# Single block pairs in the triangular inverse, a halved last doubling, opening loads in fewer pieces and moved activations

## The chip, the cores and the metric

One core of a Trainium2 chip runs the whole program once; the metric is the device time of that run in microseconds. The matrix work is done by TensorE (PE in the profile; PEld is its weight load), element work by VectorE (DVE), ScalarE (ACT) and a little by GpSimd (POOL). Transfers from device memory are issued by SyncE (SP) and by ScalarE.

## The reference

A sequence of 256 tokens of width 1024 goes through two layers of one kind and one layer of another, all in float32:

```python
for l in range(2):
    h = rms_norm(x, norm_mix[l]); proj = h @ w_in[l]          # 12 dilated heads, 4 stick-breaking heads, gates
    y_a = dilated_attention(dq, dk, dv) @ w_proj_a[l]
    y_b = stick_breaking_attention(sq, sk, sv) @ w_proj_b[l]
    x = x + (gates_a * y_a + gates_b * y_b) @ w_out[l]
    x = x + conv_ffn(rms_norm(x, norm_ffn[l]), ...)           # 1024 -> 2*2816 -> 1024
x = rms_norm(x, norm_final)
proj = rmsnorm(x) @ w_in_2
...
i_plus_a = a_low + eye(64)                                    # gated delta rule, chunks of 64 tokens, 4 heads
sol = triangular_solve(i_plus_a, rhs, lower=True)
...
mix = concat([rmsnorm(o, gdn_norm_w) * silu(z), lru_out])     # delta rule and RG-LRU
x = x + mix @ w_out_2
x = x + relu(rmsnorm(x) @ w_ff1) ** 2 @ w_ff2
return rmsnorm(x, final_norm_w)
```

## The kernel before

Every large product is made of three matmuls in a reduced float format: the weights and the streamed activations are each split into a rounded part and the rest, `wh` and `wl` for weights, `xh` and `xl` for activations. A weight block of 1 MB comes by one transfer into `raw` (L135); ScalarE writes `wh` as the rounded copy (L148, 128x1024), VectorE writes `wl = raw - wh` (L149), and PE then runs `wh*xh`, `wh*xl`, `wl*xh`. The helper `three` (L164, L165, L166) streams 256 columns (the tokens) past a 128x128 weight block; `mm_feat` runs it for 4 output blocks over 8 input blocks, 96 matmuls a call. `mm_pair` (L199, L200) does the same work as one 512-column and one 256-column matmul; `mm_tok` (L213 to L215) takes the activations as weights and streams 512 columns of `wh`. "Mains" below are the matmuls of `three`.

The tile `xx` holds the normalised activations, split, for the 8 input blocks; `xh = xx[:, :, 0]` and `xl = xx[:, :, 1]`. It is taken anew by `new_x` for each norm, in the pool `xp`, in which `x` lies ahead of it. The pools lie in SBUF one behind another in the order in which they are opened, so a larger `xx` shifts what is allocated after it: the scratch of the norms, the attention's and the gates' tiles, the FFN's `gh` and `gl`, and all tiles of the second block.

The program is written in dependency order, and a scheduler fixes one static order for each engine at build time; each engine then runs its list in order and waits by semaphores. A second tool to place work is the `mid` callback of `mm_feat` and the list `steps` with `due(i)`, which put the parts of the delta-rule solver between input blocks of a product.

The opening: the first weight quarter (2 x 1 MB) comes in eight pieces of 256 KB that alternate on SP's queue with the eight 128 KB pieces of `x`; ScalarE and VectorE split `x` and the weights piece by piece (L287, L288, L291, L292), and the sums of squares for the norm (L231) stand between them. The first product is `ps3 = mm_feat(w_first, ...)`.

In a layer, `rope_in` evacuates a q/k product by ScalarE, `rope` turns it by VectorE (L405, L411) and GpSimd, `stick(0)` and `stick(1)` start the stick-breaking scores `z` (L453).

The solver inverts `I + A` for chunks of 64 tokens in pairs (128x128 blocks, 4 heads, two batches b). `solve_base` inverts the small diagonal blocks, `level(n)` doubles: with `W` the inverse so far and `Tr` its transpose, `Y = -A * W` of the block columns (L927, masked by L930), then `Z = Tr * Y` (L935) is subtracted from `W` (L937), then `W` is transposed (L948) into `Tr` (L949). At the last n only `Tr` is updated (L941, L943). These products are plain float32, two passes a matmul in the trace, so 8 matmuls (4 heads, 2 batches) show as x16. n=2 doubles 32 to 64, n=3 doubles 64 to 128.

The end of the delta rule: for each half j of the heads, `po` (L1047, L1049) is made, squared by ScalarE (L1053), added to `q2s` (L1054), summed over features by a matmul with ones (L1058, 128x512), turned into a reciprocal root by ScalarE (L123 twice, L1063) and VectorE (L1061, L1065 to L1067), and split into `mgh` (L291) and `mgl` (L292; both show as `w`). PE meanwhile runs `out_part` on `mhl`, `mll` (96 mains), whose second half needs `mgh`, `mgl`.

Of the kernel before, what the change touches and what calls it, by code (L numbers as in the profile page):

```python
# [8 lines left out]
F32 = mybir.dt.float32  # L9
# [7 lines left out]
P = 128  # L17
T = 256
# [57 lines left out]
def kernel_body(tc, I, O, tap=lambda *a: None, upto=99):  # L76
# [3 lines left out]
    with ctx:  # L80
# [15 lines left out]
        pos_i = nrm.tile([P, T], I32, name="pos_i", tag="rb", bufs=2)  # L96
        S.dma_start(vec[:, 0:8], I["vec"][:, 0:8])
# [33 lines left out]
        def load(ap, pieces=1, between=()):  # L131
            raw = rawp.tile([P, 2048], F32, name="raw")
            n = 2048 // pieces
            for j in range(pieces):
                D.dma_start(raw[:, n * j:n * j + n], ap[:, n * j:n * j + n])  # L135
                if between:
                    between.pop(0)()
            return raw
# [156 lines left out]
        def new_x():  # L295
            xx = xp.tile([P, KB, 2, T], F32R, name="xx", tag="xx")
            return xx[:, :, 0], xx[:, :, 1], xx
# [8 lines left out]
        first = [lambda j=j: D.dma_start(x[:, j:j + 1], I["xT"][:, j:j + 1]) for j in range(8)]  # L306
        raws = [load(I["w_in"][0, 3, :, 2048 * j:2048 * j + 2048], 4, first) for j in range(2)]
        xh, xl, xx = new_x()
# [55 lines left out]
        def layer1(l, xh, xl, xx, nm):  # L364
            with tc.tile_pool(name="gt", bufs=1) as gt:
# [5 lines left out]
                with tc.tile_pool(name="at", bufs=1, reuse_waits="tile") as at, \  # L371
# [28 lines left out]
                    def rope(c, q0):  # L400
                        for j in range(2):
# [7 lines left out]
                            else:  # L409
                                pair = lambda a: a.rearrange("p m (a b) -> p m a b", b=2)  # L410
                                V.tensor_tensor(o.rearrange("p m (b a) -> p m a b", b=2), pair(q), pair(r), op=OP.add)  # L411
# [8 lines left out]
                    w0 = unit(I["w_in"][l, 0, :, 0:2048])  # L420
                    if l == 0:
                        D.dma_start(cf, I["cf"])
                    col = rstd_cols(nm, 1e-5, ab, last_lo[0] if AFT else None, parity=True)
# [49 lines left out]
                    stick(0)  # L473
                    q1 = rope_in(1, ps1)
                    ps2 = mm_feat(chunk_w(I["w_in"][l, 2]), xh, xl)
                    rope(1, q1)
                    stick(1)
                    q2 = rope_in(2, ps2)
                    ps4 = mm_tok(chunk_w(I["w_in"][l, 4]), xh, xl)
# [112 lines left out]
            with tc.tile_pool(name="ff", bufs=2) as ff, \  # L592
# [57 lines left out]
                xh, xl, xx = new_x()  # L650
# [48 lines left out]
        with tc.tile_pool(name="g1", bufs=1, reuse_waits="tile") as g1, \  # L699
# [218 lines left out]
            def level(n):  # L918
# [4 lines left out]
                for b in range(2):  # L923
                    dg = NP_[:, :, 256 * b:256 * b + 128]
                    py = bank((P, 4, 64))
                    for h in range(4):
                        PE.matmul(kr(py)[:, h], dg[:, h], ev(W[b])[:, h], start=True, stop=True,  # L927
                                  skip_group_check=True)
                    Y.append(g1.tile([P, 4, 64], F32, name="Y", tag="Y", bufs=2))
                    V.tensor_tensor(Y[b], py, lvl[n], op=OP.mult)  # L930
                for b in range(2):
                    if n < 6 - LB:
# [398 lines left out]
```

## Time and profile before

| | us |
|---|---|
| median of 3 runs (1042.63 to 1044.05) | 1042.65 |
| profiled execution, its own time | 1043.3 |
| its span in the trace | 1041.2 |
| PE busy in the span | 1028.8 |
| DVE busy | 825.0 |
| ACT busy | 609.2 |

The granted TensorE clock is 0.999 of full over the whole span. Times in the trace are counted from the start of the span; 2.1 us of the execution's time lie outside it.

### The profile page before, as it was taken

How to read it: one execution, taken by the hardware profiler on the slowest of the kernel's cores; microseconds unless marked ns; L12 is line 12 of the kernel's file. 1: busy time of each engine (PE TensorE's matmuls, PEld its weight loads, DVE VectorE, ACT ScalarE, POOL GpSimd, SP SyncE). 2: the span in 40 equal slices, each digit the busy share in tenths (PEclk: the TensorE clock that was granted, in tenths of full speed). 3: DMA queues.
4: the chain of work that ended last, by engine and by line, in shares of the span. 5: the costliest groups of instructions: out<-in, count | busy, mean ns of one | idle time of the engine just before them, and what ended most of it. 6: DMA issues, size and time to landing. Idle time of an engine off the chain costs nothing.

```text
span 1041.2 us, 17297 instructions
## 1 busy us (share of the span) xinstructions
PE 1028.8 (99%) x6950; PEld 934.2 (90%) x6950; DVE 825.0 (79%) x1390; ACT 609.2 (59%) x920; POOL 33.3 (3%) x29
## 2 busy tenths in 40 slices
PE   8999999999999999999999999999999999999997
PEld 7987899899999999878999999999999999888886
DVE  6796678978787878866989877879897998676573
ACT  5556766656556655666666565558648564454452
POOL 1320000000000002100000000000000000000000
PEclk9999999999999999999999999999999999999999
DMA  9553447455464654624455646456433245455541
GB/s 319 177 191 132 163 162 243 128 196 203 164 217 167 222 181 154 206 82 162 161 173 195 219 164 223 172 193 201 164 124 114 82 142 192 173 174 212 181 162 41
DMA packets 28257, 180.31 MB, mean 173 GB/s; under 512 B 3409, under 2 KB 5073, under 8 KB 7185
## 3 DMA queue, kind: packets, MB, share of 16 engines
q1 hardware_dynamic: 27360, 177.90, 49.4%
q10 hardware_dynamic: 816, 1.32, 0.5%
q8 instruction: 54, 0.88, 0.4%
q14 instruction: 27, 0.21, 0.1%
HBM read 177.36 MB, written 1.05 MB: 171 GB/s over the span
## 4 chain that ended last, share of the span: by engine, by line
PE 91%; DVE 5%; DMA 2%; ACT 1%; issue 1%; SPq 0%
PE ps L199 25%; PE ps L200 13%; PE acc L1102 7%; PE ps L166 7%; PE ps L164 7%; PE ps L165 7%; PE acc L165 4%; PE acc L166 4%; PE acc L164 4%; DVE wl L149 2%; PE ps L213 1%; PE ps L214 1%; PE ps L215 1%; DMA raw<-in_w_in 1%; PE acc L1171 1%; PE o L547 1%
## 5 line engine op out<-in xcount | busy, mean ns | idle before, releaser
L149 DVE TENSOR_TENSOR wl<-raw,wh 128x1024 fp32r<-128x1024 f32 x328 | 390.7, 1221 | 41.8 <-PE acc L1102 23.6
L199 PE MATMUL ps<-xx,wh 128*128 128x512 f32 x1184 | 415.9, 394 | 0.0
L148 ACT ACTIVATE wh<-raw 128x1024 fp32r<-128x1024 f32 x328 | 332.7, 1052 | 106.8 <-PE ps L165 54.2
L200 PE MATMUL ps<-xx,wl 128*128 128x256 f32 x1184 | 331.7, 281 | 0.0
L199 PEld LDWEIGHTS ps<-xx,wh 128*128 128x128 f32 x1184 | 221.4, 187 | 48.2 <-DVE t__9760 L1138 0.2
L200 PEld LDWEIGHTS ps<-xx,wl 128*128 128x128 f32 x1184 | 223.7, 189 | 2.0 <-issue 0.3
L164 PE MATMUL ps<-xx,wh 128*128 128x256 f32 x480 | 137.7, 288 | 0.8 <-ACT xx L287 0.8
L165 PE MATMUL ps<-xx,wh 128*128 128x256 f32 x480 | 136.4, 285 | 0.6 <-DVE xx L288 0.5
L166 PE MATMUL ps<-xx,wl 128*128 128x256 f32 x480 | 136.2, 285 | 0.6 <-DVE wl L149 0.5
L165 PE MATMUL acc<-gl,wh 128*128 128x256 f32 x352 | 98.7, 280 | 0.1
L164 PE MATMUL acc<-gh,wh 128*128 128x256 f32 x352 | 98.5, 280 | 0.0
L166 PE MATMUL acc<-gh,wl 128*128 128x256 f32 x352 | 98.5, 280 | 0.0
L164 PEld LDWEIGHTS ps<-xx,wh 128*128 128x128 f32 x480 | 91.8, 191 | 3.0 <-ACT xx L287 1.9
L165 PEld LDWEIGHTS ps<-xx,wh 128*128 128x128 f32 x480 | 91.9, 192 | 1.3 <-DVE xx L288 1.2
L166 PEld LDWEIGHTS ps<-xx,wl 128*128 128x128 f32 x480 | 91.6, 191 | 1.3 <-DVE wl L149 1.2
L616 ACT ACTIVATE lo<-ps 128x256 f32<-128x256 f32 x88 | 33.3, 380 | 59.9 <-PE ps L200 59.8
L164 PEld LDWEIGHTS acc<-gh,wh 128*128 128x128 f32 x352 | 66.1, 188 | 0.8
L165 PEld LDWEIGHTS acc<-gl,wh 128*128 128x128 f32 x352 | 66.2, 188 | 0.5 <-DVE gl L292 0.5
L166 PEld LDWEIGHTS acc<-gh,wl 128*128 128x128 f32 x352 | 66.2, 188 | 0.0
L634 DVE SCALAR_TENSOR_TENSOR cy<-au,vec,cy 128x256 f32<-128x256 f32 x88 | 41.9, 483 | 26.1 <-ACT cy L631 24.8
L617 DVE TENSOR_TENSOR lo<-ps,lo 128x256 f32<-128x256 f32 x88 | 37.0, 422 | 20.4 <-ACT lo L616 19.0
L631 ACT ACTIVATE cy<-au,vec 128x256 f32<-128x256 f32 x44 | 26.0, 600 | 37.4 <-DVE au L618 37.4
(452 smaller groups left out, 1582.0 us busy)
## 6 DMA issues: line engine op xcount, KB each, us to landing
raw<-in_w_in SPq DMA_DIRECT2D x50, 1024.0 KB
raw<-in_w_up SPq DMA_DIRECT2D x44, 1024.0 KB
raw<-in_w_ff SPq DMA_DIRECT2D x32, 1024.0 KB
raw<-in_w_down SPq DMA_DIRECT2D x22, 1024.0 KB
raw<-in_w_out SPq DMA_DIRECT2D x12, 1024.0 KB
raw<-in_w_proj SPq DMA_DIRECT2D x4, 1024.0 KB
raw<-in_w_in SPq DMA_DIRECT2D x8, 256.0 KB
x<-in_xT SPq DMA_DIRECT2D x8, 128.0 KB
```

What stands on the lines that cost most here:

```text
L148: S.activation(h, raw[:, j:j + 1024], AF.Copy)
L149: last_lo[0] = V.tensor_tensor(lo, raw[:, j:j + 1024], h.bitcast(F32), op=OP.subtract)
L164: PE.matmul(out, wh, xh, start=start, stop=False, skip_group_check=True)
L165: PE.matmul(out, wh, xl, start=False, stop=False, skip_group_check=True)
L166: PE.matmul(out, wl, xh, start=False, stop=stop, skip_group_check=True)
L199: PE.matmul(o, wh[:, c], xx[:, kb], start=kb == 0, stop=False, skip_group_check=True)
L200: PE.matmul(o[:, 1], wl[:, c], xx[:, kb, 0], start=False, stop=kb == KB - 1, skip_group_check=True)
L616: S.activation(lo, ps[2 * j + i][:, 1], AF.Copy)
L617: V.tensor_tensor(lo, ps[2 * j + i][:, 0], lo, op=OP.add)
L631: S.activation(y[:, j], au[:, j, 2:], AF.Identity, scale=vc("conv_w", f + 2), bias=vc("conv_b", l * 22 + 2 * c + j))
L634: V.scalar_tensor_tensor(y[:, j], au[:, j, k:k + T], vc("conv_w", f + k), y[:, j], op0=OP.mult, op1=OP.add)
L1102: PE.matmul(o, g_[:, kb, ts], w_[:, js], start=False, stop=c == 7 and kb == 3 and n == 2, skip_group_check=True)
```

## The change

Four things are changed.

1. `level(n)`: at n=2 the products for the 64-blocks are made pair by pair with 32x32 weights and 32 streamed columns (`Y` for each pair k, then `Z`), and 32-partition copies and subtractions take the place of the masked 128-partition ones. At n=3 only the lower halves are used: 64x64 weights for `Y`, and 64 rows of `Tr` and `Y` for `Z`.
2. The opening loads: the first weight quarter in five transfers (256, 256, 512, 512 and 512 KB) and `x` in three (block 0 and blocks 1 to 3 by ScalarE's queue, blocks 4 to 7 by SP's). `cf` is loaded before `w0`.
3. `new_x(off)`: `xx` becomes 160 bytes a partition longer; for the inputs of the mixer products it starts 160 bytes further in, for the FFN inputs at the old place. All pools opened after `xp` shift by 160 bytes.
4. In layer1 the calls of `rope_in(1, ...)` and `rope_in(2, ...)` stand after the next product instead of before it, and the add of `rope` is done per 64-row block, 128x256 twice for 128x512 once, over 5 of its 6 calls a layer.

```diff
+        S.dma_start(x[:, 0:1], I["xT"][:, 0:1])
         S.dma_start(vec[:, 0:8], I["vec"][:, 0:8])
...
-        def new_x():
-            xx = xp.tile([P, KB, 2, T], F32R, name="xx", tag="xx")
+        def new_x(off=0):
+            xx = xp.tile([P, KB * 2 * T + 40], F32R, name="xx", tag="xx")[:, off:off + KB * 2 * T].rearrange(
+                "p (k w t) -> p k w t", k=KB, w=2)
             return xx[:, :, 0], xx[:, :, 1], xx
...
-        first = [lambda j=j: D.dma_start(x[:, j:j + 1], I["xT"][:, j:j + 1]) for j in range(8)]
-        raws = [load(I["w_in"][0, 3, :, 2048 * j:2048 * j + 2048], 4, first) for j in range(2)]
-        xh, xl, xx = new_x()
+        raws = [rawp.tile([P, 2048], F32, name="raw") for _ in range(2)]
+        for a, b, c, d in ((0, 1, 1, 4), (1, 2, 0, 0), (2, 4, 4, 8), (4, 6, 0, 0), (6, 8, 0, 0)):
+            D.dma_start(raws[a // 4][:, 512 * (a % 4):512 * (a % 4) + 512 * (b - a)],
+                        I["w_in"][0, 3, :, 512 * a:512 * b])
+            if d > c:
+                (S if c == 1 else D).dma_start(x[:, c:d], I["xT"][:, c:d])
+        xh, xl, xx = new_x(40)
...
-                                pair = lambda a: a.rearrange("p m (a b) -> p m a b", b=2)
-                                V.tensor_tensor(o.rearrange("p m (b a) -> p m a b", b=2), pair(q), pair(r), op=OP.add)
+                                for i in range(2):
+                                    pair = lambda a: a[:, i].rearrange("p (a b) -> p b a", b=2)
+                                    V.tensor_tensor(o[:, i].rearrange("p (b a) -> p b a", b=2), pair(q), pair(r),
+                                                    op=OP.add)
...
-                    w0 = unit(I["w_in"][l, 0, :, 0:2048])
                     if l == 0:
                         D.dma_start(cf, I["cf"])
+                    w0 = unit(I["w_in"][l, 0, :, 0:2048])
...
+                    ps2 = mm_feat(chunk_w(I["w_in"][l, 2]), xh, xl)
                     q1 = rope_in(1, ps1)
-                    ps2 = mm_feat(chunk_w(I["w_in"][l, 2]), xh, xl)
                     rope(1, q1)
                     stick(1)
+                    ps4 = mm_tok(chunk_w(I["w_in"][l, 4]), xh, xl)
                     q2 = rope_in(2, ps2)
-                    ps4 = mm_tok(chunk_w(I["w_in"][l, 4]), xh, xl)
...
+                    Y.append(g1.tile([P, 4, 64], F32, name="Y", tag="Y", bufs=2))
+                    if n == 6 - LB:
+                        for h in range(4):
+                            PE.matmul(py[64:128, h], dg[0:64, h, 64:128], W[b][0:64, h, 0:64], start=True, stop=True,
+                                      skip_group_check=True)
+                        V.tensor_copy(Y[b][64:128], py[64:128])
+                        continue
+                    if n == 5 - LB:
+                        for k in range(2):
+                            e, o = slice(64 * k, 64 * k + 32), slice(64 * k + 32, 64 * k + 64)
+                            for h in range(4):
+                                PE.matmul(kr(py)[o, h, k], dg[e, h, o], W[b][e, h, e], start=True, stop=True,
+                                          skip_group_check=True)
...
+                            V.tensor_copy(kr(Y[b])[o, :, k], kr(py)[o, :, k])
+                        continue
...
+                    if n == 5 - LB:
+                        pz = bank((P, 4, 64))
...
+                                PE.matmul(kr(pz)[o, h, k], Tr[b][o, h, o], kr(Y[b])[o, h, k], start=True, stop=True,
+                                          skip_group_check=True)
...
+                            V.tensor_tensor(W[b][o, :, e], W[b][o, :, e], kr(pz)[o, :, k], op=OP.subtract)
...
-                            PE.matmul(pz[:, h], Y[b][:, h], Tr[b][:, h, 64:128], start=True, stop=True,
+                            PE.matmul(pz[:, h], Y[b][64:128, h], Tr[b][64:128, h, 64:128], start=True, stop=True,
```

The lines of the changed kernel are numbered differently: L164 to L166 become L161 to L163, L1047 and L1049 become L1080 and L1082, L1058 becomes L1091, L948 becomes L981.

**The order on PE at n=2 and n=3 of the solver.** PE's list before, from the first `Y` product of n=2 to the last `Z` product of n=3 (`g` is the solver's PSUM bank, `NP` holds A, the mains between are those of `psl`; an "x4" is four heads):

```order
L927 MATMUL g<-w_8383,NP 128x64 x4
L927 MATMUL g<-w_8392,NP 128x64 x4
...
L935 MATMUL g<-Y,w_8376 128x64 x4
L935 MATMUL g<-Y,w_8385 128x64 x4
...
L927 MATMUL g<-w_8383,NP 128x64 x4
L927 MATMUL g<-w_8392,NP 128x64 x4
...
L941 MATMUL g<-w_8376,Y 64x64 x4
L941 MATMUL g<-w_8385,Y 64x64 x4
```

The same piece of PE's list in the changed kernel:

```order
L944 MATMUL g<-w_8385,NP 32x32 x8
L944 MATMUL g<-w_8394,NP 32x32 x8
...
L960 MATMUL g<-Y,w_8378 32x32 x4
L163 MATMUL ps<-xx,wl 128x256
L960 MATMUL g<-Y,w_8378 32x32 x4
...
L935 MATMUL g<-w_8385,NP 64x64 x4
L162 MATMUL ps<-xx,wh 128x256
...
L935 MATMUL g<-w_8394,NP 64x64 x4
...
L974 MATMUL g<-w_8378,Y 64x64 x4
L974 MATMUL g<-w_8387,Y 64x64 x4
```

Before there are four places where PE leaves the mains for solver products of these two levels, three of them with full 128x128 weights; now there are eight (one for `Y` and four for `Z` at n=2, two for `Y` and one for `Z` at n=3), all with small weights and with one to seven mains between them.

**The order on PE at the gated norm.** PE's list before, from the first feature sum (L1058) to the first mains on `mgh` (`w_9215`) and `mgl` (`w_9216`); the "..." before the second L1058 stands for 20 more mains on `mhl` and `mll`, the second for 2 more:

```order
L1058 MATMUL g<-w_9222,cf 128x512
L1047 MATMUL g<-Em,w_9111 128x256
L1049 MATMUL g<-Em,w_9118 128x128
L1047 MATMUL g<-Em,w_9111 128x256
L1049 MATMUL g<-Em,w_9118 128x128
L164 MATMUL ps<-mhl,wh 128x256
...
L1058 MATMUL g<-w_9246,cf 128x512
L164 MATMUL ps<-mhl,wh 128x256
...
L164 MATMUL ps<-w_9215,wh 128x256 x4
L165 MATMUL ps<-w_9216,wh 128x256
```

The same piece in the changed kernel (nothing is left out; `mgh` is `w_9237`, `mgl` is `w_9238`):

```order
L1091 MATMUL g<-w_9244,cf 128x512
L1080 MATMUL g<-Em,w_9133 128x256
L1082 MATMUL g<-Em,w_9140 128x128
L1080 MATMUL g<-Em,w_9133 128x256
L1082 MATMUL g<-Em,w_9140 128x128
L162 MATMUL ps<-mll,wh 128x256
L163 MATMUL ps<-mhl,wl 128x256
L1091 MATMUL g<-w_9268,cf 128x512
L161 MATMUL ps<-w_9237,wh 128x256 x4
L162 MATMUL ps<-w_9238,wh 128x256
```

Between the first feature sum and the first main on `mgh` stood 24 mains, now 2; the others have moved ahead of the first feature sum, where 39 mains stand between `po` of the first half and it, for 21 before.

**The order on ACT in the opening.** ACT's list before, after its one small load (`xx` is `xh` of one block, `wh` half an entry of weights, `acc` and `sq` the squares):

```order
L115 ACT_TABLE_LOAD
L291 ACTIVATE wh<-raw 128x512
L287 ACTIVATE xx<-x,vec 128x256
L291 ACTIVATE wh<-raw 128x512
L287 ACTIVATE xx<-x,vec 128x256
L231 ACTIVATE acc<-x 128x512
```

ACT's list in the changed kernel from its start:

```order
L97 DMA x<-in_xT 128x256
L98 DMA vec<-in_vec 128x8
L116 ACT_TABLE_LOAD
L310 DMA x<-in_xT 128x768
L284 ACTIVATE xx<-x,vec 128x256
L288 ACTIVATE wh<-raw 128x512 x3
L284 ACTIVATE xx<-x,vec 128x256 x3
L288 ACTIVATE wh<-raw 128x512
```

The second block of `xx` now stands behind the third piece of `wh`; before it stood behind the second. The squares have moved behind all of these.

## Rows read from the trace of the kernel before

**Rows 1.** The page: the span, and busy time by engine.

```profile
span 1041.2 us, 17297 instructions
PE 1028.8 (99%) x6950; PEld 934.2 (90%) x6950; DVE 825.0 (79%) x1390; ACT 609.2 (59%) x920; POOL 33.3 (3%) x29
```

**Rows 2.** Waits of PE: total us, times, longest.

```profile
PE ps L213 <- ACT wh L148: 1.2, 1, 1.2
PE ps L164 <- ACT xx L287: 0.8, 2, 0.6
```

**Rows 3.** Timeline of PE and ACT in the opening: start, us, what.

```profile
7.70 0.38 PE L164 MATMUL ps<-xx,wh 128*128 128x256 f32 x1 [0.58 <-ACT xx L287]
19.50 1.05 PE L264 MATMUL ab<-cf,acc 128*128 128x4 f32 x8 [0.44 <-DMA cf<-in_cf]
6.62 0.63 ACT L291 ACTIVATE wh<-raw 128x512 fp32r<-128x512 f32 x1 [1.67 <-DMA raw<-in_w_in]
7.15 0.49 ACT L287 ACTIVATE xx<-x,vec 128x256 fp32r<-128x256 f32 x1
```

**Rows 4.** Page, bandwidth in 40 slices of the span (26 us each).

```profile
GB/s 319 177 191 132 163 162 243 128 196 203 164 217 167 222 181 154 206 82 162 161 173 195 219 164 223 172 193 201 164 124 114 82 142 192 173 174 212 181 162 41
```

**Rows 5.** Timeline of PE at solver levels n=2 and n=3.

```profile
803.70 1.90 PE L927 MATMUL g<-w,NP 128*128 128x64 f32 x16
805.40 0.36 PE L164 MATMUL ps<-xx,wh 128*128 128x256 f32 x1
...
811.48 0.28 PE L165 MATMUL ps<-xx,wh 128*128 128x256 f32 x1
811.69 1.15 PE L941 MATMUL g<-w,Y 128*64 128x64 f32 x16
...
812.99 0.28 PE L164 MATMUL ps<-xx,wh 128*128 128x256 f32 x1
```

**Rows 6.** Timeline of PE at the gated norm, to the last main on mgh and mgl.

```profile
836.73 1.02 PE L1058 MATMUL g<-w,cf 128*128 128x512 f32 x2
837.59 0.59 PE L1047 MATMUL g<-Em,w 128*128 128x256 f32 x2
...
838.82 0.36 PE L164 MATMUL ps<-mhl,wh 128*128 128x256 f32 x1
...
842.59 0.63 PE L164 MATMUL ps<-w,wh 128*128 128x256 f32 x4
843.38 0.38 PE L165 MATMUL ps<-w,wh 128*128 128x256 f32 x1 [0.16 <-DVE w L292]
...
854.10 0.28 PE L166 MATMUL ps<-w,wl 128*128 128x256 f32 x1
```

**Rows 7.** Timeline of ACT, then of DVE, at the gated norm.

```profile
839.17 0.63 ACT L1063 ACTIVATE w<-w 128x512 f32<-128x512 f32 x1
841.77 0.63 ACT L291 ACTIVATE w<-w 128x512 fp32r<-128x512 f32 x1 [1.48 <-DVE w L1067]
...
840.45 0.68 DVE L1054 TENSOR_TENSOR w<-w,w 128x512 f32<-128x512 f32 x1
842.65 0.68 DVE L292 TENSOR_TENSOR w<-w,w 128x512 fp32r<-128x512 f32 x1
```

**Rows 8.** Timeline of PE: first and last of 96 mains on xx, then of 48 on gh.

```profile
364.36 0.28 PE L164 MATMUL ps<-xx,wh 128*128 128x256 f32 x1
375.74 0.28 PE L166 MATMUL ps<-xx,wl 128*128 128x256 f32 x1
...
572.02 0.28 PE L164 MATMUL acc<-gh,wh 128*128 128x256 f32 x1
577.54 0.28 PE L166 MATMUL acc<-gh,wl 128*128 128x256 f32 x1
```

**Rows 9.** Page, groups of instructions: mains on xx and on gh, with their counts.

```profile
L164 PE MATMUL ps<-xx,wh 128*128 128x256 f32 x480 | 137.7, 288 | 0.8 <-ACT xx L287 0.8
L164 PE MATMUL acc<-gh,wh 128*128 128x256 f32 x352 | 98.5, 280 | 0.0
```

More of the change, by code (lines that the diff above doesn't have):

```diff
@@ L128, in kernel_body, with load @@
         act_set("silu_and_others")
-        def load(ap, pieces=1, between=()):
+        def load(ap):
             raw = rawp.tile([P, 2048], F32, name="raw")
[L133 to L137, printed above, removed]
+            D.dma_start(raw, ap)
             return raw
@@ L649, in layer1 @@
                 nm = Norm()
-                xh, xl, xx = new_x()
+                xh, xl, xx = new_x(40)
                 if l + 1 < L:
@@ L925, in level @@
                     py = bank((P, 4, 64))
+                    Y.append(g1.tile([P, 4, 64], F32, name="Y", tag="Y", bufs=2))
[11 more added lines that the diff above has]
+                                          skip_group_check=True)
+                        for k in range(2):
+                            o = slice(64 * k + 32, 64 * k + 64)
+                            V.tensor_copy(kr(Y[b])[o, :, k], kr(py)[o, :, k])
+                        continue
                     for h in range(4):
@@ L928, in level @@
                                   skip_group_check=True)
-                    Y.append(g1.tile([P, 4, 64], F32, name="Y", tag="Y", bufs=2))
                     V.tensor_tensor(Y[b], py, lvl[n], op=OP.mult)
                 for b in range(2):
-                    if n < 6 - LB:
+                    if n == 5 - LB:
+                        pz = bank((P, 4, 64))
+                        for k in range(2):
+                            e, o = slice(64 * k, 64 * k + 32), slice(64 * k + 32, 64 * k + 64)
+                            for h in range(4):
+                                PE.matmul(kr(pz)[o, h, k], Tr[b][o, h, o], kr(Y[b])[o, h, k], start=True, stop=True,
+                                          skip_group_check=True)
+                        for k in range(2):
+                            e, o = slice(64 * k, 64 * k + 32), slice(64 * k + 32, 64 * k + 64)
+                            V.tensor_tensor(W[b][o, :, e], W[b][o, :, e], kr(pz)[o, :, k], op=OP.subtract)
+                    elif n < 6 - LB:
                         pz = bank((P, 4, 64))
```

## The prediction

> **What bounds the kernel now.** I read the page first: PE is busy 1028.8 of 1041.2 us, DVE 825.0, ACT 609.2 [rows 1]. So the time is PE's list of matmuls plus some 12 us in which PE waits. An edit counts only if it shortens a matmul, takes matmuls away, or moves a wait of PE. The waits came next: the longest single one is 1.2 us, on ScalarE's copy of a weight block before `mm_tok`; the opening has two on `xx`, together 0.8 [rows 2]. Little is to be had from waits, and any order that adds one has to pay in full. Then the timeline: in a full stretch on `xx`, 96 mains take 375.74 - 364.36 = 11.38 us, 119.8 ns from start to start; 48 mains of the same shape on `gh` take 5.52 us, 117.4 ns [rows 8]. PE runs through both without a wait, so the 2.4 ns belong to the matmul itself. Times below are made against the profiled execution, 1043.3 us, which is 0.65 above the median of 1042.65; I take 0.65 off at the end. A change below 0.2% (2.1 us) can't be told from none.
>
> **The gated norm.** The clearest term is one that nobody wrote into the diff: the order on PE there. Call T the start of the first feature sum, 836.73 today. From it hangs a chain: its matmul (to 837.59, 0.86 long), three ScalarE steps of which the last starts at 839.17, VectorE's steps, among them the add for the second half at 840.45, ScalarE's rounding into `mgh` at 841.77, VectorE's rest `mgl` at 842.65, and the first main that needs `mgl`, at 843.38 [rows 6, 7]. That is T + 6.65. PE's own work in that time: the feature sum, the second `po` (838.82 - 837.59 = 1.23), 24 mains, the second feature sum, four mains on `mgh`, which ends about 0.3 us before 843.38; so PE waits 0.3 today. In the changed order 22 of the 24 mains stand ahead of T. What is left behind it is 0.86 + 1.23 + 2 x 0.12 + 0.86 + 4 x 0.12 = 3.7 us, while neither ScalarE's nor VectorE's steps of the chain become fewer: the second feature sum has to wait for the add (840.45 + 0.6, or T + 4.3), the mains on `mgh` for the rounding, the next for `mgl`. So PE waits about 6.65 - 3.7 = 2.95 us, 2.6 more than now. The total of mains is the same, so nothing gives it back. Bounds: 0 if the chain found 3 us that I don't see, +3.5 if VectorE, which now has a weight block's `wl` ahead of the second half's `mgl`, makes that late too. I take +2.6.
>
> **The tile `xx`.** It moves by 160 bytes for the mixer inputs. There are 3 x 480 mains on it [rows 9], 1440; 96 of them, the calls on an FFN input, stay. `gh`, which starts today 160 bytes past a multiple of 512, runs at 117.4 ns, `xx`, at a multiple, at 119.8. If the place decides, 1344 mains gain 2.4 ns each: -3.2 us. If something else does (which bank, which neighbours are at work), 0. The nearest row is that of `gh`, because it stands where `xx` will stand, so I take -3.2. But everything behind `xp` shifts as well, `gh` among it: 3 x 352 mains [rows 9] could go to 119.8, +2.5 us, or gain a little. No row shows a tile at its new place; the tile of the gated norm, another 128 bytes on, ran 93 mains from 843.38 to 854.10, 10.72 us or 116.5 ns a step [rows 6]. So I take 0 for `gh`, with -1 and +2.5 as ends.
>
> **The solver.** Before: a group of 16 passes with 128x128 weights takes 805.40 - 803.70 = 1.70 us; there are three such in n=2 and n=3. The group with 64 streamed rows and 64 weight columns, two mains with it, takes 812.99 - 811.48 = 1.51, so 1.27 without the two mains at 0.12 [rows 5]. Together 6.4 us. Entering that group costs 0.09 more than a main's step (811.69 - 811.48 = 0.21); I estimate as much for leaving it, which makes 0.19 a visit and (1.27 - 0.19) / 16 = 0.067 us a pass. After: 64 passes of 32x32 and 32 of 64x64 in eight visits. At 0.067 for all it is 6.4 + 1.5 = 7.9 us, a loss of 1.5. If a 32x32 pass costs a quarter of the 0.106 of a full one, 64 x 0.027 + 32 x 0.067 + 1.5 = 5.4, a gain of 1.0. I take 0. VectorE's copies and subtractions double in number at half the size; in the list five or more mains cover them, and a wait there would be a few tenths. The Trainium skill speaks against this part too: TensorEngine Tiling (Array Packing), Key Properties, says that changing the tiling mode drains TensorE. The trace agrees with 0.09 us on entering; by the rule alone, eight visits for one would be 7 x 0.19 = 1.3 us of loss and the smaller passes have to win that back.
>
> **The opening.** First to start is no better: `vec` now follows `x` on ScalarE's queue. The second input block starts at 7.70 now; ScalarE takes 0.53 us to a piece of `wh` (6.62 to 7.15) and 0.49 to a piece of `xx` [rows 3]. In the changed list the second `xx` stands behind the third `wh`, whose data are in a 512 KB transfer, behind 1.0 MB of others. At the 319 GB/s of the first slice [rows 4] these 1.57 MB take 4.9 us; with some 3 us before the stream runs, they land at 8 (7.5 to 9.5), and the second block starts 1.0 later, at 9.0 (8.5 to 10.5). From there 84 mains at 0.12 take 10.1, so the first product ends at 19.1 (18.6 to 20.6), against 19.06 now, where PE begins to wait for `cf` [rows 3]. Behind it the larger packets bring `cf` and `w0` earlier: the 0.44 wait on `cf` goes, perhaps 0.3 on the first `wl`. Sum: -0.2, ends -1.2 and +1.7.
>
> **Layer 0 attention.** The 1.2 us wait before `mm_tok` [rows 2] stays, as ScalarE's evacuation of `q` still stands before the weight copy; but PE's list now has two `z` groups instead of the transposes to put in front. I take half of it, -0.6 (-1.2 to +0.3). Layer 1 keeps its order. VectorE's smaller adds lie beside PE's work: nothing.
>
> **The sum.** +2.6 - 3.2 + 0 - 0.2 - 0.6 = -1.4, so 1041.9 profiled and 1041.2 as a median.
>
> **The rivals.**
> - *Place in SBUF means nothing.* `xx` stays at 119.8 ns, the wait at the gated norm stays: -1.4 + 3.2 = +1.8, 1044.5. For it: `gh` also differs from `xx` in bank and neighbours; against it, the 2.4 ns hold in every long stretch I looked at. The Trainium skill states it so: SBUF — State Buffer, in "two separate sides", says that PE never waits on another engine's access. The trace neither shows nor excludes that here. 0.21.
> - *The shift hurts what stands well* (slower). `xx` gains nothing and `gh` goes from 117.4 to 119.8: +1.8 + 2.5 = +4.3, 1046.9. It decides as soon as more than about a tenth of `gh`'s 2.4 ns is lost while `xx` gains nothing. For it: the one place of which a row shows 117.4 is left by `gh`; against it, the tile 128 bytes on is at 116.5. 0.10.
> - *The small passes overlap* (faster). If products in different corners of the array run beside each other, passes at half of the low prices, the two levels come to 3.4 instead of 6.4 us: -4.4, 1038.3. For it: the four products of a 32x32 pair group have disjoint rows and columns in twos; against it, no group of before does it. The same page lists that tiles run independently. 0.20.
> - *The change does not do what it says*: the smaller products are at 0.067 a pass and the visits eat the rest, +1.5 on the forecast, 1042.7. 0.05.
>
> **How the numbers follow.** The forecast has 0.44, its own range 1039 to 1043.5 from the ends of opening, attention and solver, which fall partly together; 0.16 of it lies below 1040.5, 0.28 within 0.2%. With the rivals: faster 0.16 + 0.20 = 0.36; same 0.28 + 0.13 (place means nothing) + 0.05 = 0.46; slower 0.08 + 0.10 = 0.18. Leaving out a tenth at each side gives 1037.8 to 1045.5.
>
> **What would show it.** The wait: in the changed profile PE stands about 2 us before the second feature sum and 0.4 to 0.5 each before the mains on `mgh` and `mgl`. The place: 96 mains on `xx` without a wait in 11.27 us or less. `gh`: 48 mains in 5.52. The solver: eight visits with steps of 0.2 at their edges, and passes between 0.03 and 0.07. The opening: the second block near 9.0 and no wait on `cf`. I am wrong if `xx` stays at 119.8, if the wait at the gated norm does not come, or if the opening starts its second block after 10.5.

## The result: 0.7% slower

Over four executions each the changed kernel took 1050.2 us (1048.31 to 1051.72) and the kernel before 1043.04 (1042.63 to 1044.05): a ratio of 1.0071, 95% interval 1.0058 to 1.0084. Forecast were 1041.2 us and a range that ended at 1045.5. On a second chip, in the experiments below, the ratio was 1.0093 (1.0061 to 1.0126), and the executions of the changed kernel spread from 1048.4 to 1056.8.

The page of the changed kernel, whose profiled execution took 1048.31 us, the fastest of the four: its span, and busy time by engine, to be read against [rows 1].

```profile
span 1046.3 us, 17369 instructions
PE 1030.1 (98%) x6982; PEld 931.5 (89%) x6982; DVE 824.0 (79%) x1404; ACT 608.6 (58%) x920; POOL 36.7 (4%) x29
```

PE's busy time grew by 1.3 us, the span by 5.1: most of what this execution lost is in waits, and the 1.9 us by which the median lies above it are not in its profile. These are PE's waits in the changed kernel (total us, times, longest; against [rows 2]):

```profile
PE ps L161 <- ACT wh L288: 2.8, 1, 2.8
PE g L1091 <- DVE w L1087: 2.0, 1, 2.0
PE ps L212 <- DVE wl L146: 1.6, 1, 1.6
...
PE g L854 <- ACT w L124: 1.1, 1, 1.1
```

The first is the opening, the second the feature sum of the gated norm, the third stands before `mm_tok` where 1.2 us stood before, and the fourth is new and was not forecast: the product of `gram` shortly ahead of the gated norm.

To see where the time goes, the mains are matched by their number in PE's list (here with the matmuls of `mm_pair`, `mm_tok` and the down products of the second block, 6224 in all), so that the hundredth of one kernel is compared with the hundredth of the other (start in us before, start after, difference; worked out from the two timelines):

```
main    before   after    after - before
   0      5.00    7.61     +2.6   first main
 100     21.25   21.61     +0.4
1000    176.03  175.92     -0.1   layer 0 without its FFN
2100    342.36  342.36      0.0
4800    756.58  755.56     -1.0   second block, ahead of the solver's last levels
5100    822.04  820.52     -1.5   behind the solver
5200    844.89  848.48     +3.6   behind the gated norm
5400    870.36  873.79     +3.4
6200   1029.09 1034.20     +5.1   end of the second block's FFN
```

The loss has two places: 5.1 us between the solver and the end of the gated norm, 1.7 us in the second block's FFN; ahead of them the change stands 1.5 ahead. Only differences between rows of this table can be read as gain or loss: profiles with one and the same opening loads are up to 2.3 us apart at the hundredth main (18.94 us in that of d_small below, 21.25 in the kernel before). Of the 1.5, the last 0.5 arose in the solver.

**The gated norm, after.** Timeline of PE in the changed kernel: start, us, what, with the idle time ahead (mains on `mhl` and `mll` left out).

```profile
831.22 0.70 PE L854 MATMUL g<-w,w 128*128 128x256 f32 x2 [1.08 <-ACT w L124]
...
839.07 1.03 PE L1091 MATMUL g<-w,cf 128*128 128x512 f32 x2
839.94 0.59 PE L1080 MATMUL g<-Em,w 128*128 128x256 f32 x2
...
843.65 1.10 PE L1091 MATMUL g<-w,cf 128*128 128x512 f32 x2 [2.00 <-DVE w L1087]
844.82 0.84 PE L161 MATMUL ps<-w,wh 128*128 128x256 f32 x4
845.76 0.58 PE L162 MATMUL ps<-w,wh 128*128 128x256 f32 x1
846.13 0.42 PE L163 MATMUL ps<-w,wl 128*128 128x256 f32 x1
...
848.48 0.39 PE L163 MATMUL ps<-w,wl 128*128 128x256 f32 x1
848.70 0.29 PE L161 MATMUL ps<-w,wh 128*128 128x256 f32 x1
848.83 0.28 PE L162 MATMUL ps<-w,wh 128*128 128x256 f32 x1
```

The chain from the first feature sum to the first main on `mgl` is 845.76 - 839.07 = 6.69 us, against 6.65 in [rows 6]: it did not shorten, and PE waits 2.0 us in the middle of it and, by the starts, 0.3 before the mains on `mgh` and 0.4 before those on `mgl`, 0.7 at its end. But behind it the mains run at (848.70 - 846.13) / 12 = 0.214 us a step, not at 0.117. The granted clock says why. Busy time by engine in five stretches of the changed kernel (us, busy of PE, PEld, DVE, ACT, POOL with counts, granted clock, DMA share, GB/s):

```profile
839.00:841.00 2.00, 2.00 (x11) 1.45 (x10) 2.00 (x6) 0.82 (x2) 0.00 (x0) 1.00 1.03 410
841.00:843.60 2.60, 0.65 (x5) 0.42 (x4) 2.60 (x6) 2.55 (x4) 0.00 (x0) 1.00 0.71 290
844.80:846.80 2.00, 1.89 (x9) 1.58 (x10) 2.00 (x4) 1.94 (x3) 0.00 (x0) 0.62 0.00 0
846.80:848.70 1.90, 1.90 (x11) 1.90 (x11) 1.90 (x5) 0.00 (x0) 0.00 (x0) 0.50 0.03 9
848.70:851.00 2.30, 2.30 (x22) 2.30 (x21) 1.79 (x3) 1.16 (x2) 0.00 (x0) 1.00 0.00 0
```

PE rests for 2 us, and then TensorE works at half speed (the granted clock is 0.50, the lower of its two levels, 1.2 instead of 2.4 GHz) for some 3 us; 13 steps from 845.76 to 848.70 take 2.94 us where at full clock they take 1.6. So the 5.1 us are 1.1 (wait of `gram`) + 2.7 (2.0 and 0.7 of wait) + 1.3 (half clock), less 0.3 of wait that stood there before [rows 6], and 0.3 of edges. The wait of `gram` too comes from a list in another order: ScalarE's has a weight copy directly ahead of the step that PE waits for, and the copy itself waits for PE; before, that step (L123) had no copy directly ahead of it. ACT's timeline before, and behind the dots in the changed kernel:

```profile
830.08 0.63 ACT L123 ACTIVATE w<-w 128x512 f32<-128x512 f32 x1 [1.96 <-DVE w L696]
...
829.59 1.06 ACT L145 ACTIVATE wh<-raw 128x1024 fp32r<-128x1024 f32 x1 [3.67 <-PE ps L162]
830.56 0.61 ACT L124 ACTIVATE w<-w 128x512 f32<-128x512 f32 x1
```

**The steps on `xx` and `gh`, after.** First and last of 96 mains on `xx`, then of 48 on `gh`, in the changed kernel; the same stretches as in [rows 8].

```profile
364.38 0.28 PE L161 MATMUL ps<-xx,wh 128*128 128x256 f32 x1
375.52 0.28 PE L163 MATMUL ps<-xx,wl 128*128 128x256 f32 x1
...
571.41 0.28 PE L161 MATMUL acc<-gh,wh 128*128 128x256 f32 x1
576.95 0.28 PE L163 MATMUL acc<-gh,wl 128*128 128x256 f32 x1
```

In this stretch `xx` went from 119.8 to 11.14 / 95 = 117.3 ns, as forecast; `gh` from 117.4 to 5.54 / 47 = 117.9. Over all mains on `xx` that follow one another the mean step went from 119.8 to 118.0, so 1440 mains gained 2.6 us and not 3.2.

**The solver, after.** PE's timeline at the first group of n=2 in the changed kernel: 32 passes, then the next main.

```profile
802.81 0.89 PE L944 MATMUL g<-w,NP 32*32 32x32 f32 x32
803.63 0.39 PE L161 MATMUL ps<-xx,wh 128*128 128x256 f32 x1
```

### The profile page after: what moved, and what is told of

It is laid out like the page before. It is cut to its first block, busy times and chain, and to the rows that moved or that the text cites. A ratio compares the mean times of both kernels' runs of the same rounds, so it can differ in the third digit from the quotient of the medians.

```text
span 1046.3 us, 17369 instructions
## 1 busy us (share of the span) xinstructions
PE 1030.1 (98%) x6982; PEld 931.5 (89%) x6982; DVE 824.0 (79%) x1404; ACT 608.6 (58%) x920; POOL 36.7 (4%) x29
## 4 chain that ended last, share of the span: by engine, by line
PE 91%; DVE 5%; DMA 1%; issue 1%; ACT 1%; POOL 0%; ACTq 0%; DVEq 0%; POOLq 0%
PE ps L196 25%; PE ps L197 13%; PE acc L1135 7%; PE ps L161 7%; PE ps L162 7%; PE ps L163 7%; PE acc L161 4%; PE acc L162 4%; PE acc L163 4%; DVE wl L146 2%; PE ps L212 1%; PE ps L211 1%; PE ps L210 1%; PE acc L1204 1%; PE o L552 1%
## 5 line engine op out<-in xcount | busy, mean ns | idle before, releaser
L161 PE MATMUL ps<-xx,wh 128*128 128x256 f32 x480 | 137.9, 288 | 2.8 <-ACT wh L288 2.8
L163 PE MATMUL ps<-xx,wl 128*128 128x256 f32 x480 | 136.4, 285 | 0.0
L161 PE MATMUL acc<-gh,wh 128*128 128x256 f32 x352 | 98.7, 280 | 0.0
L163 PE MATMUL acc<-gh,wl 128*128 128x256 f32 x352 | 98.4, 280 | 0.0
L161 PEld LDWEIGHTS ps<-xx,wh 128*128 128x128 f32 x480 | 91.6, 191 | 4.7 <-ACT wh L288 3.7
L163 PEld LDWEIGHTS ps<-xx,wl 128*128 128x128 f32 x480 | 91.5, 191 | 0.1
L161 PEld LDWEIGHTS acc<-gh,wh 128*128 128x128 f32 x352 | 66.1, 188 | 0.9
L163 PEld LDWEIGHTS acc<-gh,wl 128*128 128x128 f32 x352 | 66.3, 188 | 0.0
```

What stands on the lines that cost most here:

```text
L161: PE.matmul(out, wh, xh, start=start, stop=False, skip_group_check=True)
L163: PE.matmul(out, wl, xh, start=False, stop=stop, skip_group_check=True)
```

## The experiments

All runs compare with the kernel before on the same chip. "The change's order" is 39 and 2 mains at the gated norm, "the old order" 21 and 24.

**after_again: the changed kernel, unedited, a second time.**

> The changed kernel once more, unedited, for a second profile on the chip on which the other runs of this group are made. If what costs the time is fixed (the order at the gated norm, the shift of the tiles), the profile shows the same waits of 1.1, 2.0 and 0.7 us there and the same steps on gh in the second block's FFN, and the time is within 1 us of 1050. If the clock falls at different places from run to run, the runs differ by 2 to 6 us and with them the mean granted clock.

Measured: 1051.03 us (1048.4 to 1056.82) against 1042.44, ratio 1.0093. Both readings hold: the waits of 1.1, 2.0 and 1.6 us stand in the profile again, and the executions differ by 8 us, with mean granted clocks of 0.999, 0.999, 0.996 and, for the slowest, 0.993. The one at 0.996 is the fastest and the profiled one, and its half clock lies in the opening (0.50 from 8 to 10 us), not at the gated norm. So there is a fixed loss, present at 0.999 too (1050.92 and 1051.13 us); one that comes with the clock beside it is the reading for the slowest execution, of which no trace is kept.

**b_solver: the kernel before with the edit of `level` alone** (the hunks in `level`, no other).

> The kernel before with the edit of the solver alone. Its order on PE at the gated norm is that of the changed kernel (39 and 2 mains). If that order costs the time, this alone is slower than before by 4 to 5 us, less 0.5 that the smaller products gain: about 1046.8. If the loss comes from opening, shift or moved rope, it is within 1 us of 1043.

Measured: 1047.12 us (1046.84 to 1053.34) against 1041.54, ratio 1.0065 (1.0041 to 1.0089). The solver's edit alone brings the change's order at the gated norm, and most of the loss. In its profile the mains gain 0.5 us over the solver and lose 5.0 over the gated norm, as in the changed kernel; the same waits of 2.0 (feature sum) and 1.1 us (`gram`) are there. The slowest execution, 1053.34, has a mean clock of 0.992, the others 0.997 to 0.999; the one at 0.999 took 1046.88 us and the profiled one, with the half clock at the gated norm in it, 1047.35, so most of the loss is there without a fall of the clock.

**b_late: the kernel before with the change's order alone.** One dependency on VectorE (`los` is the list of its weight splits), no arithmetic changed; PE's list becomes 39 and 6 mains.

```diff
-                V.tensor_tensor(sq, sq, q2s[j], op=OP.add)
+                sqa = V.tensor_tensor(sq, sq, q2s[j], op=OP.add)
+                if j == 0:
+                    tc.add_manual_dep(sqa.ins, los[-1].ins.name, NOSYNC, reason="order")
```

> The kernel before with one dependency added and no arithmetic changed: the add for the first feature sum stands behind the last weight split on VectorE, which makes PE's list at the gated norm 39 and 6 mains. If that order alone costs the time, PE waits about 2.2 us longer there, and where the clock falls behind the wait another 1.9 us: 2 to 4.5 us slower than before. If the loss in the run with the solver alone came from its small products, this is within 1 us of before.

Measured: 1044.59 us against 1042.6, ratio 1.0022 (1.0013 to 1.0032), 2.0 us slower. The wait at the second feature sum is 1.5 us in its profile, and no execution shows a low clock (0.998 or 0.999 in all ten). So the order costs by its wait, without any small product. Over the gated norm its mains lose 2.3 us and those of b_solver 5.0; what b_solver has there and b_late has not is the wait of `gram`, 1.1, a second wait longer by 0.5, and the fall of the clock.

**b_half: the kernel before with the halved last doubling alone**, no 32x32 products; the order becomes 30 and 18 mains.

> The kernel before with the halved last doubling alone, no 32x32 products; PE's list at the gated norm becomes 30 and 18 mains. By the wait's arithmetic the wait there is 0.3 + 6 x 0.12 = 1.0 us, so +0.7, less 0.3 for the halved level: +0.4, the same as before within its uncertainty, and no run with a half clock in the solver. If the solver's edit as such (either level) is what costs, it is slower by 2 us or more.

Measured: 1042.55 us against 1042.6, ratio 0.9999 (0.999 to 1.0009); mean clock 0.998 or 0.999 in all ten executions. Halving the last level is free and gains nothing that can be told.

**a_order: the changed kernel with the old order.** Two weight splits (`late_lo`) are held behind the add, `for lo_ in late_lo: tc.add_manual_dep(lo_.ins, sqa.ins.name, NOSYNC, reason="order")`, which gives 20 and 21 mains.

> The changed kernel with two of VectorE's weight splits held behind the add for the first feature sum, so that PE's list at the gated norm is again 20 and 21 mains around the two feature sums; all else is the change. If the moved feature sum costs the time (2.7 us of waits and about 1.9 us of mains at half clock behind them), the stretch from the first po to the end of the mains on mgh is 4.5 to 5 us shorter and the median falls from 1050.2 to about 1045.5, no half-clock stretch there. If the solver's small products or the shifted tiles cost it, the median stays within 1 us of 1050.

Measured: 1054.42 us (1050.83 to 1055.29) against 1041.54, ratio 1.0119. My theory failed here as it stood: the wait at the second feature sum fell from 2.0 to 0.8 us, the mains lost 2.7 us over the gated norm instead of 5.1, and yet the kernel was slower than the changed one. The profile shows a loss at another place, from the last of the 32x32 products on, where PE does not wait at all. Busy time by engine in stretches of this run (columns as above):

```profile
804.00:806.00 2.00, 2.00 (x42) 1.79 (x42) 1.18 (x3) 0.93 (x2) 0.00 (x0) 1.00 0.92 258
806.00:808.00 2.00, 2.00 (x24) 1.56 (x23) 1.05 (x4) 1.06 (x1) 0.00 (x0) 1.00 0.63 266
808.00:810.00 2.00, 2.00 (x20) 1.63 (x20) 0.71 (x3) 0.00 (x0) 0.00 (x0) 0.62 0.00 0
810.00:812.00 2.00, 2.00 (x12) 1.99 (x10) 1.45 (x3) 0.37 (x1) 0.00 (x0) 0.50 0.00 0
...
820.00:822.00 2.00, 2.00 (x12) 2.00 (x11) 2.00 (x6) 1.31 (x2) 0.00 (x0) 0.50 0.00 0
822.00:824.00 2.00, 2.00 (x18) 2.00 (x18) 2.00 (x6) 0.49 (x2) 0.00 (x0) 0.97 0.00 0
```

From 809 to 822 TensorE runs at half clock: by the matched mains 5.4 us are lost in the solver, where the changed kernel's profile gains 0.5. PE counts as busy throughout, ahead of the fall in part with 32x32 weights and 32 streamed columns. Three of the four executions have a mean clock of 0.990 or 0.991, and these are the three slowest; the fourth has 0.995 and took 1050.83 us.

**a_fill: the changed kernel with useless products in the wait.**

```diff
+                if j == 1:
+                    for _ in range(5):
+                        PE.matmul(ps, ones, q2s[0].rearrange("p h t -> p (h t)"), start=True, stop=True)
                 PE.matmul(ps, ones, sq, start=True, stop=True)
```

> The changed kernel with five useless 128x512 products put in front of the second feature sum, where PE waits 2.0 us. If the half clock behind that wait is a consequence of PE's rest, the wait stays, the mains on mgh run at 0.117 instead of 0.213 from their start, and the median falls by 1.5 to 2.5 us. If the slow mains have another cause (the address of mgh, the float32 sum before them), they stay at 0.213 and the time stays or rises by up to 0.4 us.

Measured: 1052.74 us against 1041.54. I had mis-sized the filler: the five products took 4.3 us, not 2, so the time says nothing. What the run tells is the clock: behind the filled wait the mains on `mgh` run at 0.114 us from the first one on, and the granted clock is 1.00 through the whole stretch. One profile without a fall proves little by itself, for of the five profiles with the wait of 2.0 us, the changed kernel's and b_solver's show the fall, those of after_again, a_pad and a_warm don't. That of after_again just behind the wait (columns as above):

```profile
846.00:848.00 2.00, 1.80 (x13) 1.59 (x14) 2.00 (x4) 1.92 (x3) 0.00 (x0) 1.00 0.03 8
```

The address of `mgh` and the float32 sum are the same in these three, so they alone do not bring the fall about. That PE's rest does is likely (b_late, with a rest of 1.5 us, shows no low clock in ten executions), but not shown. What the fall costs can be read: from the 5100th to the 5200th main the two profiles with it lose 5.0 and 5.1 us, the three without it 3.9 to 4.0.

**a_warm: the changed kernel with 15 instead of 8 products before the data come** (`WU = 15`).

> The changed kernel with 15 instead of 8 products at the start before the data have come, so that PE is busy until the first main at 7.6 us. If the mains there run at 0.213 us from 7.6 to 12.4 because PE had rested 2.8 us, they run at 0.117 now, PE waits for the second block instead, and the first product ends 1 to 2 us earlier; the median falls by 0.5 to 2 us if nothing later takes it back, else by nothing. If the slow stretch has to do with the loads, it stays.

Measured: 1050.58 us (1049.88 to 1053.74) against 1041.54, the changed kernel's time within the spread of its executions. In the changed kernel's opening PE rests 2.8 us, and the mains behind it take 0.213 us a step from 7.6 to 12.25. In this run they take 0.117 from the start; but then PE waits 0.6 us for the second block of `xx`, and at the 200th main it is no earlier (35.2 against 34.9 and 35.0 in a_fill and a_order on the same chip). So here, where the data are the limit, the slow clock cost nothing.

**b_open: the kernel before with the opening loads alone.**

> The kernel before with the opening loads of the change alone. The changed kernel's first main starts at 7.6 instead of 5.0 us and is 0.4 us behind at the hundredth main. If the loads are neutral (2.6 lost at the start, 2.2 given back by the earlier second weights), the time is within 1 us of before. If the run of the changed kernel with the 512 byte length is right in that its opening and first layer are 2 us behind the kernel with xx moved alone, it is 1 to 2.5 us slower.

Measured: 1042.99 us against 1042.6, ratio 1.0006 (0.9996 to 1.0015). The first wait is 3.5 us in its profile, and nothing of it is left in the time that can be told.

**b_rope: the kernel before with the moved `rope_in` and the split adds alone.**

> The kernel before with the moved rope_in and the split adds alone. Forecast for this part was -0.6 us. If the wait of 1.6 us on wl before mm_tok that the changed kernel shows in place of the 1.2 us on wh belongs to this part, the time is within 0.7 us of before; if the loss of 2 us by the end of the first layer is its, 1.5 to 2.5 us slower.

Measured: 1041.85 us against 1042.6, ratio 0.9994 (0.9985 to 1.0004): the forecast of -0.6 us fits, but can't be told from nothing.

**a_pad, b_xx and b_shift: the place of the tiles.** `b_shift` is the kernel before with the change's own `new_x` (160 bytes longer), `b_xx` the same with 512 bytes, so that only `xx` moves within 512 bytes, and `a_pad` the changed kernel with 512 bytes:

```diff
-            xx = xp.tile([P, KB * 2 * T + 40], ...
+            xx = xp.tile([P, KB * 2 * T + 128], ...
```

> The kernel before with the new place of xx alone and the 512 byte length, so nothing else moves and the order on every engine stays. If the place of xx is what takes its mains from 119.8 to about 117.4 ns, 1344 of them gain 2.4 each and the kernel is 3.0 us (2 to 3.3) faster than before. If the gain in the changed kernel's profile came with the new order or loads, it is the same as before.

> The kernel before with the change's own edit of new_x, 160 bytes: xx at its new place and every tile behind it 160 bytes further. If the place decides for gh too, it loses 2.1 us in the second block's down products and 0.5 in the layers' against the run with 512 bytes, and ends 0.5 to 1 us faster than before. If gh's steps do not depend on its place, it equals the run with 512 bytes.

> The changed kernel with xx longer by 512 instead of 160 bytes, so that xx keeps its new place and all tiles behind it stand again as before within 512 bytes. If the shift of gh is what makes the second block's down products slower (227.8 to 233.3 ns a step, 2.1 us) and layer FFNs by 0.5 us or more, these steps go back to 227.8 and 117.4 and the time falls by 2 to 3 us. If they are slower for another reason, nothing changes.

Measured, against 1042.44: `b_xx` 1040.78 us, ratio 0.9982 (0.9973 to 0.9991); `b_shift` 1045.45, 1.0031 (1.0019 to 1.0042); `a_pad` 1046.21, 1.004 (1.0025 to 1.0055), where the unedited change had 1.0093. The place of `xx` alone wins 1.7 us, where 3.0 were expected; letting everything behind it slide by 160 bytes costs 4.7 (1045.45 - 1040.78), and costs 4.8 in the changed kernel (1051.03 - 1046.21). It is larger than I had expected of `b_shift`, which I thought to be faster.

Why `b_xx` wins less than forecast shows in the stretch of [rows 8], first and last of the same 96 mains on `xx`:

```profile
362.46 0.28 PE L164 MATMUL ps<-xx,wh 128*128 128x256 f32 x1
373.73 0.28 PE L166 MATMUL ps<-xx,wl 128*128 128x256 f32 x1
```

That is 11.27 / 95 = 118.6 ns a step, at the very place at which they take 117.3 in the changed kernel and in `a_pad`; in the eight profiles with `xx` at its old place they take 119.8. The place decides a part, then, and not all of it; over all mains on `xx` the mean of `b_xx` is 118.4. `gh` has two levels without being moved: its 48 mains of [rows 8] take 5.52 us before and 5.58 in b_late, d_small and d_full, where every tile is at the old place, and 5.54 with the shift. So no loss on `gh` in the layers can be told.

Part of the loss by the shift is in the second block's down products. First and last of 48 of them in `b_xx`:

```profile
910.58 0.40 PE L1103 MATMUL acc<-wh,gh 128*128 128x512 f32 x1
921.30 0.39 PE L1103 MATMUL acc<-wl,gh 128*128 128x512 f32 x1
```

and in `b_shift`:

```profile
913.45 0.39 PE L1103 MATMUL acc<-wh,gh 128*128 128x512 f32 x1
924.41 0.39 PE L1103 MATMUL acc<-wl,gh 128*128 128x512 f32 x1
```

10.72 / 47 = 228.1 ns a step against 10.96 / 47 = 233.2; there are 384 of them, so 2.0 us; in `a_pad` they are back at 228. Another part is at a place that did not move: in the FFNs `mm_pair` reads `xx` at its old place, and yet in some executions it takes longer in a whole layer. First and last of the same 64 matmuls of the same program, the changed kernel, in its first profile:

```profile
257.86 0.40 PE L196 MATMUL ps<-xx,wh 128*128 128x512 f32 x1
268.84 0.28 PE L197 MATMUL ps<-xx,wl 128*128 128x256 f32 x1
```

and in the profile of after_again:

```profile
258.22 0.39 PE L196 MATMUL ps<-xx,wh 128*128 128x512 f32 x1
269.40 0.28 PE L197 MATMUL ps<-xx,wl 128*128 128x256 f32 x1
```

10.98 against 11.18 us, 174.3 and 177.5 ns a step. With 704 such matmuls in a layer's FFN that is 2.2 us a layer at most, when it comes; by the matched mains a slow FFN is 1.5 to 1.6 us longer. In every profile in which the tiles behind `xx` stand at the old place (before, `b_xx`, `a_pad` and the eight others of this kind) both layers' FFNs run at the faster level; with the shift, the first layer of after_again, `b_shift`, a_order and a_warm and both layers of a_fill run at the slower one, and those of the first profile don't.

The two parts do not fill the 4.7 us. By the matched mains the profiles of `b_shift` and `b_xx` are 4.3 us apart at the end: 1.9 of that arose ahead of the hundredth main, 1.7 in the first layer's FFN, 1.5 in the second block's, and 0.8 were won between. As openings from the same loads are as far apart in other profiles, it stays open whether the shift had to do with those 1.9.

**d_small and d_full: useless products at level n=2 of the kernel before.** `d_small` adds 64 matmuls of 32x32 (128 passes), `d_full` 16 with 128x128 weights (32 passes) at the same place; the order at the gated norm is the same in both, 14 and 30 mains.

```diff
+                    if n == 5 - LB:
+                        for _ in range(4):
+                            for k in range(2):
+                                e, o = slice(64 * k, 64 * k + 32), slice(64 * k + 32, 64 * k + 64)
+                                for h in range(4):
+                                    PE.matmul(kr(py)[o, h, k], dg[e, h, o], W[b][e, h, e], start=True, stop=True,
+                                              skip_group_check=True)
```

> The kernel before with 64 useless 32x32 products added at level n=2 (128 passes, about 3.4 us at 0.026 each, overwritten by the real products). If a stretch of small products by itself lets the clock fall, nearly every run shows a half-clock stretch in the solver, with a mean granted clock of 0.990 to 0.995, and the time rises by 3.4 plus about 6 us, to 1051. If the falls in the solver of the changed kernel had another cause, the time rises by 3.4 us alone, to 1046, and the clock stays at 0.998.

> The control: the kernel before with 16 useless products with 128x128 weights and 64 streamed columns at the same place (32 passes at 0.106, 3.4 us, overwritten by the real ones), so that the level is as much longer with the same order at the gated norm, but the array is full. If small products make the clock fall, this one keeps it at 0.998 and takes 3.4 us more, 1046. If any longer solver level does it, this one falls too.

Measured, against 1042.61: `d_full` 1046.45 us, ratio 1.004 (1.0026 to 1.0053), mean clock 0.998 or 0.999 in eight of nine executions (0.995 in one, 1051.15 us); `d_small` 1048.58, ratio 1.006 (1.004 to 1.008), mean clock 0.996 or less in six of eight. The times of `d_small` follow its clock: 1044.49 and 1045.65 us at 0.998, 1048.0 to 1048.7 at 0.996, 1050.38 at 0.995, 1051.71 at 0.993, 1054.61 at 0.991. The passes themselves are cheaper than thought (both executions at 0.998 lie below the median of `d_full`). So with the small products a low clock was likely, not certain, and with full ones in their place it came once in nine. Where it fell in those executions no trace shows: the one kept of `d_small` is the fastest, at full clock.

**b_best: the parts that did not lose.** The kernel before with `xx` moved in 512 bytes and the moved `rope_in`.

> The kernel before with two parts of the change that did not lose: xx moved by 160 bytes with 512 bytes of length, so that all behind it stay, and the moved rope_in with split adds. If the parts add, 1.7 and 0.7 us faster than before, 2.4 in all, 1040.2, and clear of the 0.2% by a little. If the moved rope_in only filled a wait that the moved xx shortens too, it is as the run with xx alone.

Measured: 1039.64 us (1038.13 to 1041.83) against 1042.61, ratio 0.9967 (0.9954 to 0.9981): 3.0 us less, where 2.4 were expected, and faster than both kernels. PE's wait of 1.2 us before `mm_tok` [rows 2] is gone from its profile.

## Why the prediction was wrong

The parts add up: the ratios of `b_shift`, `b_solver`, `b_open` and `b_rope`, less one, sum to 0.31 + 0.65 + 0.06 - 0.06 = 0.96% (some 0.3 either way by their intervals), and the change has 0.93% on the second chip and 0.71% on the first. Point by point:

- **The gated norm**, forecast +2.6: the wait came as worked out, 2.7 us against 2.95, at the forecast places (2.0 before the second feature sum, 0.7 before `mgh` and `mgl`), and the chain was 6.69 us long against 6.65. The step that failed is its end, that PE simply waits there and nowhere else. ScalarE's and VectorE's lists shifted with the order and put a wait of 1.1 us on `gram`, which I had not looked for, so the stretch lost 3.9 to 4.0 us in three of five profiles; and I priced the rest of an engine by its length, where in two of the five the clock stood at half for 3 us behind it, 5.0 and 5.1 us in all.
- **The tile `xx`**, forecast -3.2 with 0 for everything behind it. The step that failed most is a term of the sum: "So I take 0 for `gh`, with -1 and +2.5 as ends" stood for everything behind `xx`, and the 160 bytes there cost 4.7 us. I counted only the layers' `gh`; the 384 down products of the second block with 2.0 us were left out, and so was that `mm_pair`, whose tile stays, has two levels, some 1.5 us a layer. For `xx` itself the direction was right and the size too large: 117.3 ns came in the changed kernel's stretch, but 118.6 in `b_xx`, which moves it alone, and 1.7 us arrived in the time. The 2.4 ns were read from one stretch each; `gh`, from which they were taken, needs 5.52 or 5.58 us for the same 48 mains at one and the same place. My rival "the shift hurts what stands well" had the sign right and a chance of 0.10; its place was wrong, as `xx` gained and no loss on `gh` in the layers can be told.
- **The solver**, forecast 0: 0.5 us faster where the clock holds, 32 passes in 0.82 us or 0.026 each, which is the lower price of the sum. The visits do cost: PE's step from a main into one of them is 0.20 to 0.31 us instead of 0.12. The rival by which the small passes overlap wanted half of that lower price and did not come true. What I had no term for is the clock: in the profile of a_order it fell from the last 32x32 products on, and the solver lost 5.4 us instead of gaining 0.5. In which executions of the changed kernel it fell there no kept trace shows.
- **The opening**, forecast -0.2: first main at 7.6 instead of 5.0, second block not at 9.0 but at 10.3 and, with the first already late and at half speed (0.213 us a step), without a wait of its own; in all +0.4 (the interval reaches from -0.4 to +1.6). Right by size, not by path: ScalarE could begin only at 6.5 us; ScalarE's first split stands until then, 3.6 us in all, for `vec`, a transfer of 4 KB that is now issued behind one of `x` and beside larger pieces of the weights.
- **Layer 0 attention**, forecast -0.6: -0.7, within the uncertainty. In the changed kernel a wait of 1.6 us on `wl` took the place of the 1.2 on `wh`; in the profiles of b_rope and b_best there is neither, and in that of b_open 1.2 on `wl`, so it comes with the loads.

What stays open: which accesses make `mm_pair` take one level or the other in a layer (no run moved the tiles one by one), why the mains on `xx` take 117.3 or 118.6 ns at one place, whether the shift reaches the opening, and what decides in which execution the clock falls, at the gated norm and behind the solver.

## What to carry to other kernels

A smaller product in a static schedule moves everything that was timed against it: look up the order on all engines behind the edit and work out the wait there. Pinning the old order took 1.2 us from the wait in a_order, but no run here shows that it pays in the whole time. Price PE's rest and its small tiles by the clock that can follow them too. Who pads one tile by 160 bytes pads all tiles behind it: round the padding so that the others keep their places, and measure the tile alone.

## What the hardware showed unexpectedly

- A matmul of 256 columns on `xx` takes 119.8 ns a step at the old place in every profile, and 160 bytes further on 117.3 or 118.6 in the same stretch; the down products take 228.1, or 233.2 with their tiles 160 bytes on; and after moving tiles that it does not read, a matmul can take 3.2 ns a step longer (174.3 to 177.5), in some executions only. The Trainium skill's SBUF — State Buffer ("SBUF: two separate sides") has PE never waiting on another engine; that is a statement on waiting and not on a tile's place. These rows neither show nor exclude it; they show that the steps differ with the place.
- TensorE's clock fell from 2.4 to 1.2 GHz in a stretch in which PE counted as fully busy, from the last of 32 small float32 matmuls (64 passes) on, for 13 us; this is one profile. In the opening of the changed kernel mains ran at 0.213 us a step for 4.6 us while the granted clock is shown as 1.00, and in the profile of after_again the same opening shows 0.50: in the first the step tells the clock, its row does not.
